# Softmax cross-entropy backward: which rows a partition holds, and how its labels get there

## The chip, the cores and the metric

The kernel runs on one core of one Trainium2 chip. The core has several engines with queues of their own: TensorE (PE), VectorE (DVE), ScalarE (ACT), GpSimd (POOL) and SyncE (SP), and 16 DMA engines that move data between the chip's main memory (HBM) and the core's own memory, which has 128 partitions. Times are device microseconds of one execution, the median of several runs; lower is better. The profile is that of one execution.

## The reference

For 8 x 1024 = 8192 rows of 8192 logits, the kernel computes the softmax of each row and subtracts 1 at the column that the row's label names:

```python
logits_max = np.max(logits, axis=-1, keepdims=True)
exp_logits = np.exp(logits - logits_max)
softmax = exp_logits / np.sum(exp_logits, axis=-1, keepdims=True)
one_hot[batch_idx, seq_idx, labels] = 1.0
return (softmax - one_hot).astype(np.float32)
```

Logits and output are float32, 268.4 MB each. Labels come in as 64-bit integers, 64 KB in all. Every logit is read once and every output written once, so 536.9 MB have to move whatever the order of the rows.

## The kernel before

The 8192 rows are cut into 64 tiles of 128 rows, one row per partition. A row is 8192 x 4 B = 32 KB, a tile 4 MB. The local memory holds six tiles: the tile `X` has `SLOTS` = 3 slots of `G` = 2 tiles each, and tile t sits in buffer k = t mod 6. The views `x_b` and `o_b` (`"(b p j) v -> b p j v"`) say which row goes where: tile t = 2b + j holds, in partition p, row 256b + 2p + j. Neighbouring partitions of one transfer are therefore two rows, 64 KB, apart in HBM, and the 128 rows of a transfer are spread over 8 MB. Within a partition the row is one contiguous run of 32 KB.

The order of work is written out by hand on each engine, with semaphores between them; all instructions pass through the helper `run`, whose call is line 66, which is why nearly every row of the profile says L66.

- SP issues all 64 loads in order (`load`). From the seventh on, a load waits for the store that empties its buffer (`put`). The sixth load waits instead for `w_iota`, since its buffer is first used for something else (below).
- VectorE does three things for each tile: the maximum of each row, negated (`row_max`, TENSOR_REDUCE), the reciprocal of the row sums (`invert`), and the last step (`subtract`, SCALAR_TENSOR_TENSOR): compare a row of column numbers (`iota`) with the row's label, and subtract the resulting 1 or 0.
- ScalarE takes the exponential with the row sum (`row_exp`), scales by the reciprocal (`row_scale`), and issues the store of the tile (`store`) on its own DMA queue, once VectorE has subtracted.
- The middle of the kernel is a loop over rounds of six tiles on VectorE and on ScalarE (lines 179 and 190); the first round on VectorE and the last tiles are written out. The last tile is scaled and subtracted in quarters and stored in halves.

VectorE's order is: reciprocal of tile t, maximum of tile t+1, subtraction of tile t. While that goes on, ScalarE scales tile t and takes the exponential of tile t+1.

Before all that there is a short start. POOL writes the column numbers as 16-bit integers into the sixth buffer (`made`), and VectorE copies them into PSUM (`iota`). The labels are loaded to 32 partitions (`lab_raw`, 2 KB each) and cast to float32 (`lab_f`). POOL makes a 32 x 32 identity (`ident`: a memset and an affine select), and TensorE transposes the labels twice, one time for each j, into the space of `iota`. VectorE copies the result to `lab`, where partition p finds the labels of its own rows, and only then may the column numbers overwrite that space (`w_iota` waits for `w_turned`).

Of the kernel before, what the change touches and what calls it, by code (L numbers as in the profile page):

```python
# [7 lines left out]
P = 128  # L8
G = 2
# [7 lines left out]
def kernel(  # L17
# [6 lines left out]
    nc = tc.nc  # L24
    fp32 = mybir.dt.float32
    i32 = mybir.dt.int32
    i16 = mybir.dt.int16
    Act = mybir.ActivationFunctionType
    Alu = mybir.AluOpType

    x_nv = logits.flatten_outer_dims()
    o_nv = out.flatten_outer_dims()
    N, V = x_nv.shape
    T = N // P
    B = T // G
    lab_bp = labels.rearrange("a b -> (a b)").rearrange("(b q) -> b q", q=G * P)
    x_b = x_nv.rearrange("(b p j) v -> b p j v", p=P, j=G)
    o_b = o_nv.rearrange("(b p j) v -> b p j v", p=P, j=G)

    const = ctx.enter_context(tc.tile_pool(name="const", bufs=1))  # L40
    psum = ctx.enter_context(tc.tile_pool(name="psum", bufs=1, space=bass.MemoryType.PSUM))


    X = const.tile([P, SLOTS, G, V], fp32)
    lab_raw = const.tile([B, G * P], labels.dtype)
    lab_f = const.tile([B, G, P], fp32)
    ident = const.tile([B, B], fp32)
    lab = const.tile([P, G, B], fp32)

    m, s, r = (const.tile([P, T], fp32, name=n) for n in ("m", "s", "r"))  # L50

    iota = psum.tile([P, V], i16)
    lab_ps = iota[:].bitcast(fp32)[:, :T].rearrange("p (j b) -> p j b", j=G)

    with tc.tile_critical(sync_engine=mybir.EngineType.DVE):  # L55
        sem = tc.alloc_semaphore
        got = [[sem(f"got{i}{q}") for q in range(2)] for i in range(SLOTS)]
        put = [[sem(f"put{i}{q}") for q in range(2)] for i in range(SLOTS)]
        lab_got, dve, pe, pool = (sem(n) for n in ("lab_got", "dve", "pe", "pool"))
        count = {}  # L60

        def run(engine, waits, counter, method, **operands):

            for w in waits[:-1]:
                engine.wait_ge(*w)
            instruction = getattr(engine, method)(**operands)  # L66
            for w in waits[-1:]:
                instruction._wait_ge(*w)
            step = 16 if method == "dma_start" else 1
            instruction.then_inc(counter, step)  # L70
            count[counter.name] = count.get(counter.name, 0) + step
            return counter, count[counter.name]


        w_raw = run(nc.scalar, [], lab_got, "dma_start", out=lab_raw[:], in_=lab_bp)
        w = run(nc.gpsimd, [], pool, "memset", ap=ident[:], constant=0.0)
        w_ident = run(
            nc.gpsimd, [w], pool, "affine_select",
            out=ident[:], in_=ident[:], compare_op=Alu.not_equal, fill=1.0,
            base=0, pattern=[[-1, B]], channel_multiplier=1,  # L80
        )

        made = X[:, SLOTS - 1, G - 1, :].bitcast(i16)[:, :V]
        w_made = run(
            nc.gpsimd, [], pool, "iota", out=made, pattern=[[1, V]], base=0, channel_multiplier=0
        )
        step = mybir.dt.size(labels.dtype) // 4
        lab32 = lab_raw[:].bitcast(i32).rearrange("b (p j s) -> b j p s", j=G, s=step)
        w_lab = run(nc.vector, [w_raw], dve, "tensor_copy", out=lab_f[:], in_=lab32[:, :, :, 0])
        for j in range(G):  # L90
            w = run(
                nc.tensor, [w_ident, w_lab], pe, "transpose",
                out=lab_ps[:, j, :], in_=lab_f[:, j, :], identity=ident[:],
            )
        w_turned = run(nc.vector, [w], dve, "tensor_copy", out=lab[:], in_=lab_ps)
        w_iota = run(
            nc.vector, [w_turned, w_made], dve, "tensor_scalar",
            out=iota[:].bitcast(i32), in0=made.bitcast(i32), scalar1=0, scalar2=None, op0=Alu.bitwise_or,
        )

# [6 lines left out]
        def slot(k):  # L107
            return X[:, k // G, k % G, :]
# [11 lines left out]
        def row_max(k, n):  # L120
            run(
                nc.vector, [(got[k // G][k % G], n)], max_of[k % G], "tensor_reduce",
                out=column(m, k), in_=slot(k), axis=mybir.AxisListType.X, op=Alu.max, negate=True,
            )

        def row_exp(k, n):
            run(
                nc.scalar, [(max_of[k % G], n)], exp_of[k % G], "activation", out=slot(k),
                in_=slot(k), func=Act.Exp, bias=column(m, k), scale=1.0, accum_out=column(s, k),
            )  # L130

        def invert(k, n):
            run(
                nc.vector, [(exp_of[k % G], n)], inv_of[k % G], "reciprocal",
                out=column(r, k), in_=column(s, k),
            )

        def row_scale(k, n, c=slice(0, V)):
            run(
                nc.scalar, [(inv_of[k % G], n)], scl_of[k % G], "activation", out=slot(k)[:, c],  # L140
                in_=slot(k)[:, c], func=Act.Copy, bias=0.0, scale=column(r, k),
            )

        def subtract(k, n, label, c=slice(0, V)):
            run(
                nc.vector, [(scl_of[k % G], n)], sub_of[k % G], "scalar_tensor_tensor",
                out=slot(k)[:, c], in0=iota[:, c], scalar=label, in1=slot(k)[:, c],
                op0=Alu.is_equal, op1=Alu.subtract, reverse1=True,
            )

        def store(k, n, target, c=slice(0, V)):
            run(
                nc.scalar, [(sub_of[k % G], n)], put[k // G][k % G], "dma_start",
                out=target[:, c], in_=slot(k)[:, c],
            )

        def counter(engine, first):
            reg = engine.alloc_register(f"from{first}")
            engine.reg_mov(reg, first)
            return reg  # L160
# [10 lines left out]
        for t in range(R):  # L171
            k, n = t % R, t // G + 1
            invert(k, n)
            row_max((k + 1) % R, 16 * ((t + 1) // R + 1))
            subtract(k, n, lab[:, t % G, t // G : t // G + 1])

        done = [counter(nc.vector, SLOTS + q + 1) for q in range(SLOTS)]
        landed = counter(nc.vector, 32)
        with nc.vector.Fori(SLOTS, ROUNDS * SLOTS, SLOTS) as b:
            for k in range(R):  # L180
                invert(k, done[k // G])
                if k == R - 1:
                    nc.vector.reg_add(landed, landed, 16)
                row_max((k + 1) % R, landed)
                subtract(k, done[k // G], lab[:, k % G, bass.ds(b + k // G, 1)])
            for reg in done:
                nc.vector.reg_add(reg, reg, SLOTS)

        done = [counter(nc.scalar, q + 1) for q in range(SLOTS)]
# [11 lines left out]
        for t in range(ROUNDS * R, T - 1):  # L201
            k, n = t % R, t // G + 1
            invert(k, n)
            row_max(k + 1, 16 * (ROUNDS + 1))
            row_scale(k, n)
            row_exp(k + 1, n + k % G)
            subtract(k, n, lab[:, t % G, t // G : t // G + 1])
            store(k, n, o_b[t // G, :, t % G, :])
        k, n = (T - 1) % R, B
        invert(k, n)  # L210
        for q in range(4):
            c = slice(q * V // 4, (q + 1) * V // 4)
            row_scale(k, n, c)
            subtract(k, n + q, lab[:, G - 1, B - 1 : B], c)
        half = V // 2
        store(k, n + 1, o_b[B - 1, :, G - 1, :], slice(0, half))
        stored = {}
# [38 lines left out]
```

## Time and profile before

| | |
|---|---|
| time, median of 3 runs | 1247.37 us (1247.26 to 1247.46) |
| time of the profiled execution | 1247.37 us |
| its span, first to last instruction | 1245.6 us |
| VectorE busy | 1122.8 us, 90% |
| ScalarE busy | 919.3 us, 74% |
| bytes moved by DMA | 536.96 MB, mean 431 GB/s |
| loads of 4 MB: number, median from issue to landing | 64, 24.2 us |
| stores of 4 MB: number, median from issue to landing | 63, 55.2 us |

How to read it: each row of slices cuts the span into 40 equal parts and shows the busy share in tenths; the DMA row is the mean over the 16 DMA engines. q1 is the queue on which SP issues the loads, q10 that on which ScalarE issues the stores; both use the same 16 DMA engines, and the share behind each is the time that its packets took, as a share of the 16 engines' span. A waits row names the waiting engine and line, what it waited for, and the total, the number and the longest of the waits in us. SPq and ACTq are the issuing sides of the DMA queues. Rows of a time line give start and length in us, engine, line, operation, what is written and what is read, and in brackets the idle time before and what ended it.

### The profile page before, as it was taken

The numbers are of one execution on the slowest core, as the hardware profiler recorded it, in microseconds if no ns is written. First come the engines' busy times: TensorE is split into PE (matmuls) and PEld (weight loads), VectorE is DVE, ScalarE is ACT, GpSimd is POOL, SyncE is SP. The second block draws the span as 40 slices with busy tenths as digits, with TensorE's granted clock in tenths as the row PEclk, the third lists the DMA queues.
The fourth block names the chain that finished last, engine by engine and source line by source line (L and its number), as shares of the span: only waits on it lengthen the run. The fifth ranks groups of instructions, "written<-read, shape, count | busy, mean of one in ns | idle before, by whom it ended". The sixth has DMA issues, their size and how long they took to land.

```text
span 1245.6 us, 863 instructions
## 1 busy us (share of the span) xinstructions
PE 0.4 (0%) x2; PEld 0.3 (0%) x2; DVE 1122.8 (90%) x198; ACT 919.3 (74%) x196; POOL 7.4 (1%) x7
## 2 busy tenths in 40 slices
PE   0000000000000000000000000000000000000000
PEld 0000000000000000000000000000000000000000
DVE  6999999999988989889898898988988989889893
ACT  3888888888767777677767777677777777777772
POOL 2000000000000000000000000000000000000000
DMA  9999999999999999999999999999999999999999
GB/s 406 416 427 437 437 430 429 438 434 428 435 438 432 427 437 438 430 429 437 437 429 430 438 432 429 435 438 431 428 437 437 431 429 437 434 431 431 437 433 395
DMA packets 18626, 536.96 MB, mean 431 GB/s; under 512 B 2080, under 2 KB 2080, under 8 KB 2112
## 3 DMA queue, kind: packets, MB, share of 16 engines
q1 hardware_dynamic: 9216, 268.44, 50.0%
q10 hardware_dynamic: 9408, 268.51, 49.9%
q14 instruction: 2, 0.02, 0.0%
HBM read 268.50 MB, written 268.44 MB: 431 GB/s over the span
## 4 chain that ended last, share of the span: by engine, by line
another core or an unknown queue 67%; DVE 22%; DMA 6%; issue 2%; SPq 1%; DVEq 0%; ACT 0%; ACTq 0%; PE 0%
DVE m L66 11%; DVE X L66 10%; DMA out_dram<-X 4%; DMA X<-in_logits_dram 2%; SPq L66 1%; DVE lab_f L66 0%; DVE iota L66 0%; DVEq L55 0%; DMA lab_raw<-in_labels_dram 0%; ACT X L66 0%; DVE r L66 0%; PE iota L66 0%; ACTq L66 0%; DVE lab L66 0%
## 5 line engine op out<-in xcount | busy, mean ns | idle before, releaser
L66 DVE TENSOR_REDUCE m<-X 128x1 f32<-128x8192 f32 x64 | 555.7, 8683 | 90.9 <-DMA X<-in_logits_dram 90.9
L66 ACT ACTIVATE X<-X,m 128x8192 f32<-128x8192 f32 x64 | 455.8, 7122 | 185.2 <-DVE m L66 185.2
L66 DVE SCALAR_TENSOR_TENSOR X<-iota,lab,X 128x8192 f32<-128x8192 int16 (+1 forms) x67 | 560.0, 8362 | 2.4 <-ACT X L66 2.4
L66 ACT ACTIVATE X<-X,r 128x8192 f32<-128x8192 f32 (+1 forms) x67 | 456.3, 6815 | 118.2 <-DVE r L66 118.2
L66 DVE RECIPROCAL r<-s 128x1 f32<-128x1 f32 x64 | 9.9, 155 | 7.3 <-ACT X L66 7.3
L66 ACT ACTIVATION_READ_ACCUMULATOR X<-X,m 128x1 f32 x64 | 11.9, 186 | 0.0
L66 DVE CAST lab_f<-lab_raw 32x256 f32<-32x256 int32 x1 | 4.8, 4778 | 3.7 <-DMA lab_raw<-in_labels_dram 3.7
L66 POOL IOTA X<- 128x8192 int16 x1 | 6.9, 6943 | 0.0
L66 DVE TENSOR_SCALAR iota<-X 128x4096 int32<-128x4096 int32 x1 | 4.4, 4428 | 0.1
L66 ACT ACT_TABLE_LOAD x1 | 1.3, 1283 | 1.4 <-DVEq L55 1.4
L66 DVE COPY lab<-iota 128x64 f32<-128x64 f32 x1 | 0.2, 225 | 0.5 <-PE iota L66 0.5
L66 PE MATMUL iota<-ident,lab_f 32*128 32x32 f32 x2 | 0.4, 300 | 8.5 <-DVE lab_f L66 8.5
L66 PEld LDWEIGHTS iota<-ident,lab_f 32*128 32x128 f32 x2 | 0.3, 196 | 8.5 <-DVE lab_f L66 8.5
L66 POOL TENSOR_SCALAR_AFFINE_SELECT ident<-ident 32x32 f32<-32x32 f32 x1 | 0.2, 203 | 0.1
L66 POOL MEMSET ident<- 32x32 f32 x1 | 0.1, 115 | 0.6 <-DVEq L55 0.6
L240 POOL MEMSET const-bfloat16-1.0<- 128x1 bf16 x1 | 0.1, 106 | 0.0
L240 POOL MEMSET const-uint8-127<- 128x1 uint8 x1 | 0.1, 106 | 0.0
L240 POOL MEMSET const-float32-0.0<- 128x1 f32 x1 | 0.1, 103 | 0.2 <-issue 0.2
L240 POOL MEMSET const-float32-1.0<- 128x1 f32 x1 | 0.1, 103 | 0.0
## 6 DMA issues: line engine op xcount, KB each, us to landing
X<-in_logits_dram SPq DMA_DIRECT2D x64, 4096.0 KB, 24.2
out_dram<-X ACTq DMA_DIRECT2D x63, 4096.0 KB, 55.2
out_dram<-X ACTq DMA_DIRECT2D x2, 2048.0 KB, 16.6
lab_raw<-in_labels_dram ACTq DMA_DIRECT2D x1, 64.0 KB, 2.7
```

Source lines behind the costliest of these rows:

```text
L66: instruction = getattr(engine, method)(**operands)
L240: nc = _bacc.Bacc("TRN2", target_bir_lowering=False, num_devices=1)
```

## The change

The rows are dealt out in another way. The views become `"(p b j) v -> b p j v"`: partition p holds the 64 consecutive rows 64p to 64p + 63, and tile t = 2b + j takes row 64p + t from each. Neighbouring partitions of a transfer are 64 rows, 2 MB, apart, and the 128 rows of a transfer are spread over the whole tensor of 268.4 MB. The size of a transfer, its number of pieces (128 of 32 KB), the queues and the waits of loads and stores are as they were.

With this order the labels of partition p are 64 consecutive numbers, so they are loaded to 128 partitions (512 B each) and cast in place. The identity, the two transposes, the copy behind them and the semaphore of TensorE go, and `w_iota` waits only for the column numbers. The label of tile t is column t of `lab`.

```diff
-    lab_bp = labels.rearrange("a b -> (a b)").rearrange("(b q) -> b q", q=G * P)
-    x_b = x_nv.rearrange("(b p j) v -> b p j v", p=P, j=G)
-    o_b = o_nv.rearrange("(b p j) v -> b p j v", p=P, j=G)
+    lab_pt = labels.rearrange("a b -> (a b)").rearrange("(p t) -> p t", p=P)
+    x_b = x_nv.rearrange("(p b j) v -> b p j v", p=P, j=G)
+    o_b = o_nv.rearrange("(p b j) v -> b p j v", p=P, j=G)
...
-    lab_raw = const.tile([B, G * P], labels.dtype)
-    lab_f = const.tile([B, G, P], fp32)
-    ident = const.tile([B, B], fp32)
-    lab = const.tile([P, G, B], fp32)
-
+    lab_raw = const.tile([P, T], labels.dtype)
+    lab = const.tile([P, T], fp32)
+
+    lab_bj = lab[:].rearrange("p (b j) -> p b j", j=G)
...
-        w_raw = run(nc.scalar, [], lab_got, "dma_start", out=lab_raw[:], in_=lab_bp)
-        w = run(nc.gpsimd, [], pool, "memset", ap=ident[:], constant=0.0)
-        w_ident = run(
-            nc.gpsimd, [w], pool, "affine_select",
-            out=ident[:], in_=ident[:], compare_op=Alu.not_equal, fill=1.0,
-            base=0, pattern=[[-1, B]], channel_multiplier=1,
-        )
-
+        w_raw = run(nc.scalar, [], lab_got, "dma_start", out=lab_raw[:], in_=lab_pt)
...
-        lab32 = lab_raw[:].bitcast(i32).rearrange("b (p j s) -> b j p s", j=G, s=step)
-        w_lab = run(nc.vector, [w_raw], dve, "tensor_copy", out=lab_f[:], in_=lab32[:, :, :, 0])
-        for j in range(G):
-            w = run(
-                nc.tensor, [w_ident, w_lab], pe, "transpose",
-                out=lab_ps[:, j, :], in_=lab_f[:, j, :], identity=ident[:],
-            )
-        w_turned = run(nc.vector, [w], dve, "tensor_copy", out=lab[:], in_=lab_ps)
+        lab32 = lab_raw[:].bitcast(i32).rearrange("p (t s) -> p t s", s=step)
+        run(nc.vector, [w_raw], dve, "tensor_copy", out=lab[:], in_=lab32[:, :, 0])
         w_iota = run(
-            nc.vector, [w_turned, w_made], dve, "tensor_scalar",
+            nc.vector, [w_made], dve, "tensor_scalar",
...
-            subtract(k, n, lab[:, t % G, t // G : t // G + 1])
+            subtract(k, n, lab[:, t : t + 1])
...
-                subtract(k, done[k // G], lab[:, k % G, bass.ds(b + k // G, 1)])
+                subtract(k, done[k // G], lab_bj[:, bass.ds(b + k // G, 1), k % G])
...
-            subtract(k, n + q, lab[:, G - 1, B - 1 : B], c)
+            subtract(k, n + q, lab[:, T - 1 : T], c)
```

More of the change, by code (lines that the diff above doesn't have):

```diff
@@ L44 @@
     X = const.tile([P, SLOTS, G, V], fp32)
-    lab_raw = const.tile([B, G * P], labels.dtype)
-    lab_f = const.tile([B, G, P], fp32)
-    ident = const.tile([B, B], fp32)
-    lab = const.tile([P, G, B], fp32)
+    lab_raw = const.tile([P, T], labels.dtype)
+    lab = const.tile([P, T], fp32)
+    lab_bj = lab[:].rearrange("p (b j) -> p b j", j=G)
     m, s, r = (const.tile([P, T], fp32, name=n) for n in ("m", "s", "r"))
     iota = psum.tile([P, V], i16)
-    lab_ps = iota[:].bitcast(fp32)[:, :T].rearrange("p (j b) -> p j b", j=G)
     with tc.tile_critical(sync_engine=mybir.EngineType.DVE):
@@ L58 @@
         put = [[sem(f"put{i}{q}") for q in range(2)] for i in range(SLOTS)]
-        lab_got, dve, pe, pool = (sem(n) for n in ("lab_got", "dve", "pe", "pool"))
+        lab_got, dve, pool = (sem(n) for n in ("lab_got", "dve", "pool"))
         count = {}
@@ L206 @@
             row_exp(k + 1, n + k % G)
-            subtract(k, n, lab[:, t % G, t // G : t // G + 1])
+            subtract(k, n, lab[:, t : t + 1])
             store(k, n, o_b[t // G, :, t % G, :])
```

## The prediction

> **What bounds the kernel now.** I read the page from the top: the busy shares, the forty slices, the queues.
>
> ```profile
> span 1245.6 us, 863 instructions
> PE 0.4 (0%) x2; PEld 0.3 (0%) x2; DVE 1122.8 (90%) x198; ACT 919.3 (74%) x196; POOL 7.4 (1%) x7
> ...
> DMA  9999999999999999999999999999999999999999
> GB/s 406 416 427 437 437 430 429 438 434 428 435 438 432 427 437 438 430 429 437 437 429 430 438 432 429 435 438 431 428 437 437 431 429 437 434 431 431 437 433 395
> ...
> q1 hardware_dynamic: 9216, 268.44, 50.0%
> q10 hardware_dynamic: 9408, 268.51, 49.9%
> ...
> HBM read 268.50 MB, written 268.44 MB: 431 GB/s over the span
> ```
>
> VectorE at 90% looks like the bound, but the DMA row has no slice below 9, and the loads (q1) and stores (q10) together fill 99.9% of the sixteen DMA engines' span. The second view is the waits, of the compute engines and of SP's queue.
>
> ```profile
> DVE m L66 <- DMA X<-in_logits_dram: 90.9, 47, 2.4
> ...
> SPq L66 <- DMA out_dram<-X: 1140.8, 58, 57.3
> ...
> SPq L66 <- DVE iota L66: 10.1, 1, 10.1
> ```
>
> VectorE waits for loads 47 times. SP waits for stores nearly all the time: a load goes out when the store that occupied its slot has landed. The third view is the chain in order of time, cut to one period.
>
> ```profile
> 322.19 18.98 another core or an unknown queue
> 341.17 0.02 issue
> 341.19 0.33 SPq L66
> 341.52 19.06 another core or an unknown queue
> ```
>
> One load and one store, 2 x 4.194 MB, pass every 341.52 - 322.19 = 19.33 us, which is 434 GB/s. The chain cannot name the wait; the queues can. Here they are in the stretch from 400 to 600 us, and below them the rate of the long middle (the last two columns are DMA share and GB/s).
>
> ```profile
> q10 hardware_dynamic: 1493, 43.68, 50.6%
> q1 hardware_dynamic: 1488, 42.99, 49.8%
> ```
>
> ```profile
> 310.00:700.00 390.00, 0.00 (x0) 0.00 (x0) 351.00 (x61) 290.47 (x61) 0.00 (x0) 1.00 1.00 434
> ```
>
> The packets that carry data are whole rows of 8192 x 4 = 32768 B (the rest of the count are tiny). On q10 43.68 MB are 1333 of them, in 50.6% of 16 x 200 us: 1.215 us each; on q1 42.99 MB are 1312, in 49.8%: 1.215 us too. The kernel moves 2 x 8192 of them, so 16384 x 1.215 / 16 = 1244.2 us of the span's 1245.6. The time is the packet time and little else. Around the span lie 1247.37 - 1245.6 = 1.8 us; the profiled execution's own time equals the median of the runs.
>
> **The change, part by part.** First the labels' path, at the start, in order of time.
>
> ```profile
> 0.96 0.42 ACTq L66 DMA_DIRECT2D lab_raw<-in_labels_dram  x1
> 1.00 0.12 POOL L66 MEMSET ident<- 32x32 f32 x1 [0.56 <-DVEq L55]
> 1.05 13.03 SPq L66 DMA_DIRECT2D X<-in_logits_dram  x6
> 1.20 0.20 POOL L66 TENSOR_SCALAR_AFFINE_SELECT ident<-ident 32x32 f32<-32x32 f32 x1
> 1.36 6.94 POOL L66 IOTA X<- 128x8192 int16 x1
> ...
> 3.67 4.78 DVE L66 CAST lab_f<-lab_raw 32x256 f32<-32x256 int32 x1 [3.67 <-DMA lab_raw<-in_labels_dram]
> ...
> 8.50 0.42 PE L66 MATMUL iota<-ident,lab_f 32*128 32x32 f32 x2 [8.50 <-DVE lab_f L66]
> 8.96 0.23 DVE L66 COPY lab<-iota 128x64 f32<-128x64 f32 x1 [0.51 <-PE iota L66]
> 9.30 4.43 DVE L66 TENSOR_SCALAR iota<-X 128x4096 int32<-128x4096 int32 x1
> 13.63 8.68 DVE L66 TENSOR_REDUCE m<-X 128x1 f32<-128x8192 f32 x1
> ```
>
> ```profile
> DMA to landing us min/median/max: 12.3/24.2/60.0
> ```
>
> Removed are the memset and the select on POOL, two weight loads and two matmuls on PE, and one copy on VectorE. POOL's iota starts 1.36 - 1.00 = 0.36 us sooner and ends near 7.94. The cast ended at 8.45, 0.15 after the iota's 8.30; whether it lasted 4.78 us because of its 256 elements or because POOL was busy, the copy into the iota tile needs both, so it starts near 8.1 instead of 9.30: 1.2 us sooner. Two things hang on it. The first maximum also needs load 0, which landed at about 1.05 + 12.3 = 13.4 (the minimum is load 0, the only one with nothing ahead), so the maximum moves by at most 0.3 us. And SP's sixth load goes out 1.2 us sooner, behind five loads that hold the engines for 5 x 4.194 MB / 434 GB/s = 48 us: worth nothing. Were that cover gone it would gain the 1.2 us. The labels' transfer keeps its 64 KB but goes to 128 partitions in pieces of 512 B instead of 32 of 2 KB. From issue to cast it took 2.7 us; doubled, the cast starts near 6.4 and the iota still ends later. Cost nothing, at worst 2 us on the first maximum, which five queued loads hide as well. In the loop the label's register offset has a step of two elements instead of one, with as many instructions in the listing: nothing, and VectorE's wait for the load covers it. No wait is added and nothing is queued behind a new one.
>
> Second, the layout. Load t took rows 256b + 2p + j and now takes 64p + 2b + j. Its 128 packets lay 64 KB apart, over 8 MB; now they lie 2 MB apart, over all 268 MB. Stores do the same. Packets keep their size, number, queues and order, so every term stays except the 1.215 us. What a packet costs at that distance no row shows. Before, the starts of packets that go side by side differed in address bits 16 to 22; now all bits below 21 are equal in the whole transfer. If the memory chooses its part by those bits, sixteen engines work at the same part whenever they are near the same offset, and a packet lengthens; engines that are already 99.9% taken hide none of it.
>
> The lower end is 1.215 us, packets untouched: 1247. For the upper the nearest rows are those of a place where all engines are taken and yet move less: from 47 to 51 us, when the sixth load and the first store begin. The columns of the first are as above; the second is the queue's own row from 47 to 50 us.
>
> ```profile
> 47.00:51.00 4.00, 0.00 (x0) 0.00 (x0) 4.00 (x2) 3.54 (x1) 0.00 (x0) 1.00 1.06 344
> 48.00:49.00 1.00, 0.00 (x0) 0.00 (x0) 1.00 (x1) 1.00 (x1) 0.00 (x0) 1.00 1.38 360
> ```
>
> ```profile
> q1 hardware_dynamic: 32, 1.05, 109.3%
> ```
>
> In 3 us two packets per engine took 109.3% of 48 engine-us (over 100%, as some end later): 52.5 / 32 = 1.64 us each, 1.35 times 1.215. The trace does not say why; it shows only by how much packets lengthen here when something holds them. As a price for every packet, 16384 x 1.64 / 16 = 1679, with 1.4 inside the span and 1.8 around it 1683. By rate instead, 536.96 MB / 344 GB/s = 1561, with the same 3 us 1564. The worst microsecond moves 360 / 1.38 = 261 GB/s per full set of engines: 2057, so 2060. From 1247 to 2060, then; no gain, except by the rival below. I take the middle of 1564 and 1683, because only these rows show sixteen engines held at once, and equal low bits concern all sixteen: **1623 us**, a period of 19.33 x 1623 / 1247 = 25.2 us.
>
> The Trainium skill, "DMA: Bandwidth & Descriptors", Latency and other measured facts, says that rows a large power of two apart in HBM slow copies down, naming 164 GB/s per direction at a pitch of 2 MiB against 214 at full rate, for 16 KiB pieces. The sum by it would be 536.96 / 328 = 1637 us, an estimate from that page, with the mechanism only inferred there. The trace's 434 GB/s, 217 each way, agrees with its full rate; that the pitch matters no row here shows.
>
> **The rivals.** *Only one direction suffers.* Loads or stores alone lengthen, say because writes are buffered. For it: the row of 47 to 50 us shows only loads lengthened. Against: both queues have the same addresses and the same 1.215 us. 8192 x (1.64 + 1.215) / 16 = 1462, with 3 us **1465**.
>
> *The memory does not care.* Both packet times are 1.215 us and the middle's rate stays at 434, so the engines, not the memory, may set the pace with memory to spare; each packet remains a contiguous 32 KB. Then only the start's 0.3 us is left and the DMA engines cover that: **1247**. Here too belongs that the layout does not act as I read it. Against: the constant packet time was got at one pitch only. The same page of the Trainium skill ("DMA: Bandwidth & Descriptors", Rules for kernel authors) asks only for 128 partitions and at least 1 MiB per DMA for full bandwidth, which both kernels satisfy; by that rule alone the time stays.
>
> *Worse than the row.* Sixteen engines at the same part might keep meeting, as in the worst microsecond: **2060**, and from 1800 up I count it here.
>
> *Faster.* The slices swing between 427 and 438 GB/s. If the dips are packets 64 KB apart that meet, and 2 MB apart they do not, every slice reaches 438: 536.96 / 438 = 1226, with 3 us **1229**. The place is the packets of the whole middle; it decides once the mean packet falls below 1.215 by 0.2%. Against: dip and peak are 2.5% apart while the two queues' packet times agree, which looks like how whole packets fall into slices.
>
> **How the numbers follow.** Both directions lengthened, 1500 to 1800: 0.55. One direction or a milder lengthening, 1290 to 1500: 0.20. Worse, 1800 to 2060: 0.12. No change: 0.10. Faster: 0.03. The range 1290 to 2060 leaves out the last two, 0.13, and some odd tail. What this kernel's measurement can tell from no change is 0.2%, 2.5 us; every lengthening above is far beyond it, so slower has 0.87.
>
> **What would show it.** Right: DMA slices stay at 9 while GB/s falls to about 330, q1 and q10 keep their megabytes and near 50% each over a longer span (packet time about 1.6 us), VectorE's wait for loads grows from 90.9 us by the 1623 - 1247 = 376 us to some 470, the long group means (the maximum, the exponential) stay. If only one direction suffers, the two shares part. At the start no matmul, and the iota copy ends near 12.5 us. Wrong: a period still at 19.3 us and packets of 1.215 us mean memory had room; DMA slices below 9 mean that something other than packet time, a queue or a slot, became the bound, which I have at nothing.

## The result and the profile after

The changed kernel takes 1331.03 us (median; 1325.94 to 1345.40), against 1247.41 us: a ratio of 1.069, 95% interval 1.0657 to 1.0723. It is slower by 84 us, where 376 were forecast. (Ratios leave out a run that took over 1.5% longer than the fastest of the same kernel, medians do not; below it concerns one run alone, 2058.68 us of the kernel with 8 KB pieces 2 MB apart.) The page of the changed kernel, with the busy times, the forty slices and the queues:

```profile
span 1324.2 us, 852 instructions
...
DVE 1123.9 (85%) x197; ACT 919.4 (69%) x196; POOL 7.2 (1%) x5
...
DMA  9999999999999999999999999999999999999997
GB/s 371 390 343 386 402 410 412 393 387 418 423 422 398 399 422 424 419 405 400 421 424 419 401 389 429 422 418 415 409 426 423 405 414 414 423 428 401 418 397 307
...
q1 hardware_dynamic: 9216, 268.44, 51.8%
q10 hardware_dynamic: 9504, 268.51, 47.5%
...
HBM read 268.50 MB, written 268.44 MB: 405 GB/s over the span
```

The shape is the forecast one: the engines stay taken (9 in every slice but the last), the megabytes are the same, and they move at 405 GB/s instead of 431. The compute engines' busy times have hardly changed (VectorE 1123.9 us against 1122.8, ScalarE 919.4 against 919.3). What has changed is the length of a packet, and not alike in the two queues. For the loads 51.8% of 16 x 1324.2 us over 8192 packets is 1.340 us; for the stores 47.5% gives 1.229. Both were 1.215. These are means. In the packets' records of the traces the usual packet still takes 1.213 us on both queues, as before; but 16% of the loads' packets take more than 1.25 times that, 1.84 us on average, where 0.4% did before. Of the stores' packets it is 1%.

VectorE feels it as longer waits for loads. Below are the waits and then the issues, with the median from issue to landing at the end of each row:

```profile
DVE m L64 <- DMA X<-in_logits_dram: 170.8, 57, 4.3
...
SPq L64 <- DMA out_dram<-X: 1212.7, 58, 68.1
```

```profile
X<-in_logits_dram SPq DMA_DIRECT2D x64, 4096.0 KB, 32.3
out_dram<-X ACTq DMA_DIRECT2D x63, 4096.0 KB, 51.3
```

The wait grew from 90.9 by 79.9 us, the span by 78.6: nearly all of the loss shows as loads that come late. A load lands after 32.3 us instead of 24.2, a store after 51.3 instead of 55.2. With later loads fewer stores are queued at a time; I read the end, where engines now run dry, as the result of that. The last two columns are DMA share and GB/s, first of the changed kernel, then of the kernel before:

```profile
1290.00:1300.00 10.00, 7.61 (x3) 8.17 (x5) 0.00 (x0) 1.00 0.80 344
...
1315.00:1320.00 5.00, 0.00 (x0) 0.00 (x0) 0.00 (x0) 1.00 0.71 256
1320.00:1324.20 4.20, 0.00 (x0) 0.00 (x0) 0.00 (x0) 1.00 0.06 27
```

```profile
1230.00:1240.00 10.00, 0.00 (x0) 0.00 (x0) 0.00 (x0) 0.00 (x0) 0.00 (x0) 1.00 0.98 419
1240.00:1245.60 5.60, 0.00 (x0) 0.00 (x0) 0.00 (x0) 0.00 (x0) 0.00 (x0) 1.00 0.57 246
```

The sixteen engines idle 2.0 + 1.5 + 3.9 = 7.4 us here, 0.2 + 2.4 = 2.6 before. So the 78.6 us of span are 8192 x 0.125 / 16 = 64 from the loads, 8192 x 0.014 / 16 = 7 from the stores, some 5 from the end, and the rest within the rounding of the shares (0.1% is 1.3 us).

The start, in order of time:

```profile
1.05 11.81 SPq L64 DMA_DIRECT2D X<-in_logits_dram  x6
1.09 6.95 POOL L64 IOTA X<- 128x8192 int16 x1 [0.65 <-DVEq L53]
...
2.97 5.12 DVE L64 CAST lab<-lab_raw 128x64 f32<-128x64 int32 x1 [2.97 <-DMA lab_raw<-in_labels_dram]
8.08 4.43 DVE L64 TENSOR_SCALAR iota<-X 128x4096 int32<-128x4096 int32 x1
16.12 8.69 DVE L64 TENSOR_REDUCE m<-X 128x1 f32<-128x8192 f32 x1 [3.62 <-DMA X<-in_logits_dram]
```

No matmul; the copy of the column numbers ends at 12.5 us instead of 13.7. The first maximum now waits 3.62 us for load 0: the gain is gone before the loop begins.

### The profile page after: what moved, and what is told of

It is laid out like the page before. It is cut to its first block, busy times and chain, and to the rows that moved or that the text cites. A ratio compares the mean times of both kernels' runs of the same rounds, so it can differ in the third digit from the quotient of the medians.

```text
span 1324.2 us, 852 instructions
## 1 busy us (share of the span) xinstructions
DVE 1123.9 (85%) x197; ACT 919.4 (69%) x196; POOL 7.2 (1%) x5
## 2 busy tenths in 40 slices
DMA packets 18722, 536.96 MB, mean 406 GB/s; under 512 B 2080, under 2 KB 2208, under 8 KB 2208
## 3 DMA queue, kind: packets, MB, share of 16 engines
q1 hardware_dynamic: 9216, 268.44, 51.8%
q10 hardware_dynamic: 9504, 268.51, 47.5%
## 4 chain that ended last, share of the span: by engine, by line
another core or an unknown queue 51%; DMA 32%; DVE 12%; issue 3%; SPq 1%; DVEq 0%; ACT 0%; ACTq 0%
DMA out_dram<-X 19%; DMA X<-in_logits_dram 13%; DVE X L64 7%; DVE m L64 5%; SPq L64 1%; DVEq L53 0%; ACT X L64 0%; DVE r L64 0%; ACTq L64 0%; DVEq L164 0%; DVEq L172 0%; ACTq L175 0%; ACTq L144 0%; SPq L236 0%
## 5 line engine op out<-in xcount | busy, mean ns | idle before, releaser
L64 DVE CAST lab<-lab_raw 128x64 f32<-128x64 int32 x1 | 5.1, 5123 | 3.0 <-DMA lab_raw<-in_labels_dram 3.0
## 6 DMA issues: line engine op xcount, KB each, us to landing
X<-in_logits_dram SPq DMA_DIRECT2D x64, 4096.0 KB, 32.3
out_dram<-X ACTq DMA_DIRECT2D x63, 4096.0 KB, 51.3
```

## The experiments

**The two parts, and the two directions.** Each kernel is the changed one with old views put back.

```diff
 labels_alone
-    x_b = x_nv.rearrange("(p b j) v -> b p j v", p=P, j=G)
-    o_b = o_nv.rearrange("(p b j) v -> b p j v", p=P, j=G)
+    x_b = x_nv.rearrange("(b p j) v -> b p j v", p=P, j=G)
+    o_b = o_nv.rearrange("(b p j) v -> b p j v", p=P, j=G)
 loads_2mb: only the line of o_b is put back
 stores_2mb: only the line of x_b is put back
```

> The new label path with the old views of logits and output (rows 64 KB apart in both directions); each row then gets the label of another row, so the output differs in the ones, and nothing else of the work changes. If all of the loss is the layout: 1247.4 us, within 0.5. If the 512 B label pieces or the later cast cost something that the queues hand on: 1250 or more.

> Loads 2 MB apart, stores 64 KB apart; the output's rows are stored in another order, the work is the same. Theory A, reads at 2 MB suffer by their own addresses: about 1320 us, with load packets at a mean of some 1.33 us and the same loads slow as in the changed kernel. Theory B, loads and stores have to meet, both at 2 MB: under 1260 us, all packets near 1.215 us. Theory C, stores at 2 MB hold the memory and the loads only show it: 1247 us.

> Loads 64 KB apart, stores 2 MB apart; the output's rows are stored in another order, the work is the same. Theory A (reads by their own addresses): 1247 to 1253 us, load packets at 1.215 us. Theory B (loads and stores meet): under 1260 us. Theory C (stores at 2 MB hold the memory): about 1320 us, with lengthened load packets although the loads are 64 KB apart.

The labels' part alone: 1247.31 us, ratio 1.000 (0.9991 to 1.001). It is worth nothing, either way. Loads alone at 2 MB: 1276.23 us, 1.0256 (1.0216 to 1.0297). Stores alone: 1270.65 us, 1.0206 (1.0171 to 1.0242). None of the three theories is right by itself: each direction costs 23 to 29 us, and together they cost 84, which is about 31 more than the sum. The queues' shares, first with the loads at 2 MB and then with the stores:

```profile
q1 hardware_dynamic: 9216, 268.44, 50.5%
q10 hardware_dynamic: 9504, 268.51, 48.8%
```

```profile
q1 hardware_dynamic: 9216, 268.44, 50.5%
q10 hardware_dynamic: 9504, 268.51, 49.3%
```

Over spans of 1274.2 and 1268.9 us these are load packets of 1.257 and 1.252 us, store packets of 1.215 and 1.222. With stores 2 MB apart the packets that lengthen are mainly those of the loads, which lie 64 KB apart there. So the queue on which time is lost does not tell which stream causes it.

**Is it the distance, or the equal addresses?** In this kernel the loads' rows lie 63 rows apart, 32 KB less than 2 MB; stores stay at 2 MB.

```diff
 loads_63_rows
-    x_b = x_nv.rearrange("(p b j) v -> b p j v", p=P, j=G)
+    x_b = x_nv[: P * 63 + 0, :].rearrange("(p q) v -> p q v", p=P)
...
-            run(nc.sync, after, got[k // G][j], "dma_start", out=slot(k), in_=x_b[b, :, j, :])
+            run(nc.sync, after, got[k // G][j], "dma_start", out=slot(k), in_=x_b[:, t, :] if t < 63 else x_nv[63 : 63 + 127 * 63 + 1 : 63, :])
```

> The changed kernel with loads whose rows lie 63 rows (2 MB less 32 KB) apart instead of 64; partitions get rows that they should not, the loads' size and number are the same, stores stay 2 MB apart. Theory F, what costs is that the addresses of one load are equal modulo 2 MB: the loads then cost what they cost at 64 KB, about 1271 us as with stores alone at 2 MB. Theory G, what costs is that a transfer touches the whole tensor, 2 MB regions each: 1325 to 1340 us.

1271.73 us, 1.0184 (1.0164 to 1.0203): what the stores alone cost, within the spread of the runs (1267.56 to 1274.49). Theory F stands for the loads: nearly the same distance, but addresses that are not equal modulo 2 MB, costs them nothing that these runs can tell. The same shows without any store. From 5 to 45 us only loads run, and these are the rates of before, of the loads at 2 MB, of the changed kernel, whose loads have the same addresses, and of the loads 63 rows apart (last two columns, DMA share and GB/s):

```profile
5.00:45.00 40.00, 0.42 (x2) 0.29 (x2) 32.09 (x7) 20.96 (x4) 3.30 (x1) 1.00 1.00 433
```

```profile
5.00:45.00 40.00, 29.28 (x6) 18.65 (x4) 3.04 (x1) 1.00 0.99 392
```

```profile
5.00:45.00 40.00, 29.10 (x6) 18.47 (x4) 3.04 (x1) 1.00 0.99 411
```

```profile
5.00:45.00 40.00, 31.71 (x6) 21.07 (x4) 3.04 (x1) 1.00 1.00 433
```

Each rate is that of one execution. Much of the loss falls on the first load: in the changed kernel the packets of the first four loads take 1.50, 1.24, 1.22 and 1.21 us on average, with the loads alone at 2 MB 1.53, 1.31, 1.31 and 1.28, before 1.25, 1.21, 1.21 and 1.21. So equal low bits lengthen some packets, and by no means all.

The stores were not tried 63 rows apart: the last tile would then write rows that the first has written.

**How it goes with the distance.** Partition p takes r consecutive rows of each chunk of 128 r rows; the two loops are written out, since the tile's place is no longer linear in b.

```diff
 pitch_1m (ROWS = 32; pitch_512k has ROWS = 16 and i=16 in the line of the labels)
-    lab_pt = labels.rearrange("a b -> (a b)").rearrange("(p t) -> p t", p=P)
+    lab_pt = labels.rearrange("a b -> (a b)").rearrange("(c p i) -> p c i", p=P, i=32)
+    ROWS = 32
+    x_cipv = x_nv.rearrange("(c p i) v -> c i p v", p=P, i=ROWS)
+    x_b = [x_cipv[t // ROWS, t % ROWS] for t in range(T)]
+    o_cipv = o_nv.rearrange("(c p i) v -> c i p v", p=P, i=ROWS)
+    o_b = [o_cipv[t // ROWS, t % ROWS] for t in range(T)]
...
-        w_raw = run(nc.scalar, [], lab_got, "dma_start", out=lab_raw[:], in_=lab_pt)
+        w_raw = run(nc.scalar, [], lab_got, "dma_start", out=lab_raw[:].rearrange("p (c i) -> p c i", i=ROWS), in_=lab_pt)
...
```

> Partition p holds 16 consecutive rows of each quarter of the tensor: packets of loads and stores lie 512 KB apart, every output is right, the two loops are written out. Theory F (equal low bits cost): between, 1255 to 1300 us. Theory G (a transfer touches the whole tensor): it now touches a quarter, 1270 us or so. If only bits from 2 MB up matter to the memory's choice: 1247 us.

> Packets 1 MB apart in both directions, loops written out, every output right. 64 KB: 1247, 512 KB: 1268, 2 MB: 1331 us. Theory F (the more low bits are equal, the more is lost): between, 1280 to 1315 us. If the 2 MB step alone makes the large loss: about 1270.

512 KB: 1267.86 us, 1.0154 (1.0110 to 1.0199). 1 MB: 1279.12 us, 1.0260 (1.0243 to 1.0278), a little under what was expected. So 0, 20, 32 and 84 us at 64 KB, 512 KB, 1 MB and 2 MB. But the edit changes the labels' path too: they now come in 512 pieces of 128 B or 256 of 256 B. These are the queues and the label cast of 512 KB, then of 1 MB; behind the cast's bar stand its busy time in us, its duration in ns and its wait:

```profile
q1 hardware_dynamic: 9216, 268.44, 49.9%
q10 hardware_dynamic: 9888, 268.51, 49.2%
...
L67 DVE CAST lab<-lab_raw 128x64 f32<-128x64 int32 x1 | 0.2, 195 | 26.2 <-DMA lab_raw<-in_labels_dram 26.2
```

```profile
q1 hardware_dynamic: 9216, 268.44, 50.3%
q10 hardware_dynamic: 9632, 268.51, 48.9%
...
L67 DVE CAST lab<-lab_raw 128x64 f32<-128x64 int32 x1 | 0.2, 194 | 15.6 <-DMA lab_raw<-in_labels_dram 15.6
```

At 512 KB the labels land only after 26.2 us, the first store goes out at 64.0 us instead of 49.5, and from 60 to 100 us the DMA engines idle for some 6 us (DMA share 0.73 up to 70 us, 0.78 up to 80, 0.94 up to 100). At 1 MB the first store goes out at 53.4 us and the engines do not run dry there. So the packet times are the cleaner measure. Over spans of 1268.1 and 1276.3 us the load packet takes 1.236 and 1.254 us, between 1.215 and 1.340, and the store packet 1.219 in both. Put as time, 8192 packets of each at 512 KB and 1 MB lose some 13 and 22 us, against 71 at 2 MB: the loss grows with the number of equal low bits, and most from the last step.

**Which loads are slow.** Grouped by load from the packets' records of the traces (load number modulo 8, from the ninth load on; mean packet in us):

```text
                0     1     2     3     4     5     6     7
changed       1.26  1.28  1.26  1.29  1.30  1.48  1.29  1.47
store_swapped 1.27  1.29  1.28  1.30  1.30  1.45  1.30  1.47
rows_moved    1.27  1.29  1.28  1.30  1.30  1.46  1.29  1.48
loads_2mb     1.24  1.24  1.25  1.24  1.25  1.25  1.25  1.25
stores_2mb    1.24  1.25  1.25  1.24  1.24  1.25  1.23  1.24
```

With both directions at 2 MB two loads in every eight are slower than the others by 0.19 us a packet; 16 such loads of 8 packets per engine make 16 x 8 x 0.19 = 24 us, most of the 31 that both lose beyond the sum of each alone. Two kernels moved the rows.

```diff
 store_swapped
-                target = o_b[bass.ds(b + k // G, 1), :, k % G, :]
+                target = o_b[bass.ds(b + k // G, 1), :, 1 - k % G, :]
...
 rows_moved (loops written out as above, ROWS = 64)
+    x_b = [x_cipv[0, t ^ 1] for t in range(T)]
+    o_b = [o_cipv[0, t ^ 4] for t in range(T)]
```

> The changed kernel with the stores of the two tiles of a pair going to each other's rows (each output row is its neighbour's; the work is the same). In the changed kernel the loads of tiles 5 and 7 modulo 8 are the slow ones (packets of about 1.48 us, the others 1.27). Theory D, a load is slow when the store beside it has a certain position relative to it: the slow loads are others than 5 and 7 modulo 8, or spread out, and the time may move by 10 us or more from 1331. Theory E, a load is slow by its own rows: still 5 and 7 modulo 8, 1331 us within 8.

> Rows 2 MB apart in both directions, loops written out; load t takes the rows that tile t with its last bit turned would take, store t writes those of t with bit 2 turned (rows are stored in another order; the work is the same). Theory E, a load is slow by its own rows: the slow loads move from 5 and 7 to 4 and 6 modulo 8, and the time stays at 1331 within 10. Theory D, by its position relative to the store beside it: another pattern. Theory N, by its place in the order of work: still 5 and 7.

1330.48 us, 1.0691 (1.0651 to 1.0731), and 1324.56 us, 1.0627 (1.0600 to 1.0653). The slow loads are 5 and 7 in both. The first kernel alone seemed to say that a load is slow by its own rows; the second, in which those loads read other rows, takes that back. Of the three theories this leaves N, their place in the order of work; a relation between the rows of loads and stores through address bits that neither kernel turned is not excluded. With 16 KB pieces (the kernel half_rows below) the same tiles are the slow ones, 0.88 and 0.89 us against 0.65 to 0.73, so the period counts tiles and not transfers. The six buffers have no period of eight, and what has stays open.

**The length of a piece.** Each tile's transfers are cut into two or four, by columns; or one load brings two tiles, as 64 KB of consecutive rows.

```diff
 half_rows (two parts; quarter_rows has four, and the counts that the waits expect grow by as much)
-            run(nc.sync, after, got[k // G][j], "dma_start", out=slot(k), in_=x_b[b, :, j, :])
+            for h in range(2):
+                c = slice(h * V // 2, (h + 1) * V // 2)
+                run(nc.sync, after * (h == 0), got[k // G][j], "dma_start", out=slot(k)[:, c], in_=x_b[b, :, j, c])
...
 row_pairs
-    x_b = x_nv.rearrange("(p b j) v -> b p j v", p=P, j=G)
+    x_b = x_nv.rearrange("(p b j) v -> b p (j v)", p=P, j=G)
...
+            if j:
+                return
+            after = after or [w_iota] * (t == R - G)
+            run(nc.sync, after, got[k // G][0], "dma_start", out=X[:, k // G, :, :].rearrange("p j v -> p (j v)"), in_=x_b[b])
...
-                nc.vector, [(got[k // G][k % G], n)], max_of[k % G], "tensor_reduce",
+                nc.vector, [(got[k // G][0], n)], max_of[k % G], "tensor_reduce",
...
 half_rows_64k, quarter_rows_64k, row_pairs_64k: the same with the old views
```

> The changed kernel with each load and each full store cut into two transfers of 128 x 16 KB, 2 MB apart as before. Theory H, the pieces' length is why the loss is 7% and not the 31% that the Trainium skill (DMA: Bandwidth & Descriptors, other measured facts) states for 16 KiB pieces at this pitch: about 1640 us. Theory I, the length of a piece does not matter: 1331 to 1350 us.

> The changed kernel with each load and each full store cut into four transfers of 128 x 8 KB. Halves took 1410 us, whole rows 1331. Theory J, a load packet loses about 0.13 us whatever its length (0.126 for 32 KB, 0.133 for 16 KB): 32768 load packets lose 266 us of the sixteen engines, with some 10 to 20 us more for the smaller packets' own cost 1530 to 1560 us. Theory K, halves cost more because twice as many transfers are issued: the loss does not double again, under 1480 us.

> The changed kernel with one load for both tiles of a pair, 128 pieces of 64 KB, 2 MB apart; stores as they were, every output right. Theory J, if the pieces become packets of 64 KB: half as many load packets, each losing 0.13 us, about 1290 us, packets at 2.4 us when undisturbed; if the packets stay at 32 KB, 1320 to 1340 us. Theory K (the number of transfers): 1290 us in both cases.

> The same cut into 16 KB pieces with the old views, 64 KB apart (each row gets another row's label, the work is the same). Theory J: no loss but the smaller packets' own cost, 32768 x 0.611 / 16 = 1251 and 3, about 1255 us, with all packets at 0.611 us. Theory K (the number of transfers costs): 1280 us or more.

> Pieces of 8 KB in four transfers per tile with the old views, 64 KB apart (each row gets another row's label; the work is the same). At 2 MB this took 2025 us. Theory L, the loss is the distance's, and grows as the pieces shrink: 32768 x 2 x 0.309 / 16 = 1266 and 3, 1265 to 1290 us, DMA engines full from the start. Theory K, four times the transfers cost by themselves: over 1500 us, engines with gaps in the first 50 us.

> One load for two tiles, packets of 64 KB, with the old views (each row gets another row's label; the work is the same). At 2 MB this took 1488 us. Theory L (the distance's): 1245 to 1265 us, load packets at 2.43 us. Theory M, a load that waits for two stores and moves 8 MB at once costs by itself: 1400 us or more.

| piece | 64 KB apart | 2 MB apart | loss |
|---|---|---|---|
| 8 KB | 1266.64 us | 2025.26 us, 1.6154 (1.6122 to 1.6186) | 759 us |
| 16 KB | 1254.66 us | 1410.03 us, 1.1304 (1.1285 to 1.1323) | 155 us |
| 32 KB | 1247.4 us | 1331.03 us, 1.069 (1.0657 to 1.0723) | 84 us |
| 64 KB (loads) | 1267.17 us | 1488.23 us, 1.1947 (1.1923 to 1.1972) | 221 us |

(The intervals are those against the kernel before.) The 64 KB column rules out theory K: twice or four times the transfers cost 7 and 19 us, no more. The loss comes with the rows 2 MB apart, as theory L has it. Theory J, a fixed loss of 0.13 us per load packet, had been read off the 32 and 16 KB pieces; it falls at 8 and at 64. The queues of the kernel with 8 KB pieces at 2 MB, and the same pieces at 64 KB:

```profile
q1 hardware_dynamic: 36864, 268.45, 65.5%
q10 hardware_dynamic: 36720, 268.52, 32.6%
```

```profile
q1 hardware_dynamic: 36864, 268.45, 50.4%
q10 hardware_dynamic: 36720, 268.52, 50.3%
```

Over 2030.5 and 1263.8 us and 32768 packets the load packet takes 0.649 us at 2 MB and 0.311 at 64 KB, the store packet 0.323 and 0.310. Loads double, stores hardly move.

**Which direction makes the short pieces slow.** Two last kernels cut to 8 KB: loads alone at 2 MB, and loads 63 rows apart with stores at 2 MB.

```diff
 quarter_loads_2mb: quarter_rows with the old line of o_b
 quarter_loads_63: quarter_rows with the loads' view of loads_63_rows
```

> 8 KB pieces, loads 2 MB apart, stores 64 KB apart (rows are stored in another order; the work is the same). Theory O, the loads carry the loss of short pieces: 1800 us or more, and 255 GB/s in the first 45 us, where no store runs. Theory P, loads and stores have to meet at 2 MB: under 1450 us.

> 8 KB pieces, loads 63 rows (2 MB less 32 KB) apart, stores 2 MB apart (partitions get rows that they should not; the work is the same). Theory F with O: the loads run as at 64 KB, 424 GB/s in the first 45 us, and what is left is the stores' part, 1270 to 1400 us. If the distance itself and not the equal low bits is what short pieces suffer from: 1800 us or more.

1401.13 us, 1.1233 (1.1186 to 1.1281), and 1531.07 us, 1.2275 (1.2131 to 1.2419). The windows from 5 to 45 us (loads only) and in the middle, of the first and of the second kernel:

```profile
5.00:45.00 40.00, 23.28 (x5) 14.34 (x3) 3.05 (x1) 1.00 0.75 256
310.00:700.00 390.00, 313.27 (x53) 258.04 (x54) 0.00 (x0) 1.00 1.01 389
```

```profile
5.00:45.00 40.00, 31.86 (x6) 21.22 (x4) 3.04 (x1) 1.00 1.01 423
310.00:700.00 390.00, 279.36 (x49) 227.28 (x49) 0.00 (x0) 1.00 1.00 347
```

At 2 MB the loads alone fall to 256 GB/s at the start, with the engines at three quarters; 63 rows apart they keep 423. The loads' equal addresses are the cause there. But in the middle the loads alone recover to 389, and the larger part of the loss comes with the stores (347). Against 1267 the loads cost 134 us, the stores 264, both 759: each makes the other dearer, as with whole rows. Theory P's time, under 1450, came true for the first kernel, but not its reason: in the second kernel stores at 2 MB cost 264 us although the loads there do not lie 2 MB apart. Theory O was right only for the start, and the second kernel lies between the two expectations.

## Why the prediction was right in kind and wrong in size

- *What bounds the kernel.* Right. The compute engines keep their busy times, and the time followed the packet time: 64 + 7 of 78.6 us of span.
- *The labels' path at nothing.* Right: 1247.31 us with it alone. Its steps came as forecast (the iota copy ended at 12.5 us); the transfer in 512 B pieces landed sooner, not later (the cast began at 2.97 us instead of 3.67).
- *The mechanism.* Right in part for the loads: equal low bits, not the distance, as the 63 rows show; but they lengthen a sixth of the loads' packets and leave the usual one at 1.213 us. For the stores it is argued from likeness; the reverse test was not made. That it is a part of the memory at which engines meet is the reading that fits, and no run shows the memory's inside.
- *The term that failed: the price of a packet.* "I take the middle of 1564 and 1683, because only these rows show sixteen engines held at once" put some 1.58 us on every packet of both queues (1620 x 16 / 16384). Measured means were 1.340 on loads and 1.229 on stores. A long packet costs what the borrowed row says, or more (1.84 us against 1.64); what failed is the step from it to every packet, for only 16% of the loads' packets and 1% of the stores' are long. The rows from 47 to 51 us show two packets per engine at one disturbance that occurs once; nothing tied them to addresses. They were the nearest rows that showed longer packets, but their nearness was in appearance only. With the measured prices the forecast's own sum, 8192 x (1.340 + 1.229) / 16, gives 1315, and 3 around it 1318; the rest of the profiled execution's 1325.94 is the idle end, 7.4 us, for which the prediction left the 1.4 us of before.
- *The rival "only one direction suffers", 1465.* Its profile came true, for the loads' packets are nearly the only ones to lengthen, while its cause did not: both directions take part, and each lengthens loads. Its place in the range, 1290 to 1500, was the one that held. Its price was the same borrowed 1.64.
- *No change, faster, worse than the row.* Out: the ratio's interval is 1.0657 to 1.0723, and the slowest run took 1345.40 us. That the swing of the slices had nothing to give was not tested by itself; 63 rows apart, loads alone run at the old 433.
- *The Trainium skill's row in "DMA: Bandwidth & Descriptors" (Latency and other measured facts).* It agrees with the runs in direction, and its 16 KiB pieces matter: 536.96 / 1410.03 us is 381 GB/s, 190 each way at 2 MB, where the page has 164; with 32 KB pieces 202. At 512 KB its 207 stands beside 536.96 MB / 1267.86 us / 2 = 212, with 32 KB pieces and the late labels in it. The estimate of 1637 from it was about as far off as the forecast.

Open remain the period of eight, how stores 2 MB apart lengthen the packets of loads that are not, why both directions together lose more than the sum, and why 64 KB pieces lose more than 32.

## What to carry to other kernels

When a kernel's time is packet time, look at the addresses that the DMA engines touch at the same moment: rows whose addresses are equal modulo a large power of two cost from 1% at 512 KB (13 us of packet time) to 7% at 2 MB with 32 KB pieces, and 60% with 8 KB pieces against the same pieces 64 KB apart, although the DMA engines show as busy nearly throughout and the compute engines do the same work. A step of one row less removed the loads' part at once; removing setup work that queued transfers hide was worth nothing. A price taken from a transient elsewhere in the trace says how long a disturbed packet can be, not how many packets are disturbed: put on every packet, it gave here a loss four and a half times too large.

## What the runs showed of the hardware that was not expected

Stores 2 MB apart lengthen mainly the loads' packets, not their own: with only the stores at 2 MB the load packet takes 1.252 us and the store packet 1.222, against 1.215 before. With 8 KB pieces at 2 MB in both directions it is 0.649 against 0.323.

The label cast lasted 5.12 us for 64 elements per partition, and 4.78 us for 256 before; both ended within 0.2 us of the end of POOL's iota (8.09 and 8.04 us, 8.45 and 8.30). So its length is not its size. The two kernels with late labels show what it is: their cast of the same 64 elements starts at 26.2 and 15.6 us, long after the iota, and lasts 0.195 and 0.194 us. So nearly all of the 5.12 us is a wait that ends with the iota. It fits the Trainium skill, "SBUF — State Buffer" (SBUF: two separate sides), by which VectorE in some of its modes and GpSimd share a pair of ports that the one that starts first holds for its whole instruction; which mode the cast had, no run here shows.

The labels themselves, 64 KB in all, landed 2.0 us after their issue in 128 pieces of 512 B, but after 14.6 us in 256 pieces of 256 B and 25.2 us in 512 pieces of 128 B, each time beside the first loads. Why is not shown.
